# A gating norm moved ahead of a weight split, one weight unit loaded earlier, and accumulator banks taken in three groups

## The chip, the cores and the metric

The kernel runs on one core of one Trainium2 chip. The metric is the time of one execution in microseconds, measured on the device. Three runs of the kernel before gave a median of 531.14 us (531.03 to 531.18). A difference of about 0.2% is the smallest that such a measurement can tell from no change.

## The reference

One decoder layer on 256 tokens of width 1024, in float32. `h` is the running sum.

```python
h = h + 0.5 * swiglu(rmsnorm(h, ffn1_norm), ...)          # hidden width 2816
n = rmsnorm(h, mix_norm)
z = n @ w_in                                              # q, k, v, u, gv, 512 columns each
attn = causal attention over 8 heads of 64 (256 tokens are one block)
zg = gelu(z[..., 1536:])                                  # u and gv
gm = u * (tril(w_s) @ layernorm(gv) + b_s)                # in chunks of 128 tokens, 8 groups
gates = sigmoid(n @ w_gate + b_gate)                      # 2048 columns
merged = gates[:, :1024] * (attn @ w_branch_attn) + gates[:, 1024:] * (gm @ w_branch_gmlp)
h = h + merged @ w_out
h = h + 0.5 * swiglu(rmsnorm(h, ffn2_norm), ...)
out = rmsnorm(h, final_norm)
```

## The kernel before, in words

Every weight is read once, in units of 1 MB, in the order in which TensorE uses them (the list `units`, lines 107 to 116): first FFN, then two units each of q, k, gv, u and v, eight of the gates, four of the branches, four of the output projection, second FFN. A unit arrives as two halves of 512 KB in a ring of seven raw buffers (`fetch_to`, line 131, issued on SyncE's queue, SP). `split_half` (line 141) turns each half into a high and a low part of a reduced float format: a copy on ScalarE (line 195), then a subtraction on VectorE (line 197). The split weights lie in a ring of four units (`wp`). Each product is three matmuls, high by high, high by low and low by high (`mm3`, lines 190 to 192).

`chunk` (line 347) asks `unit` (line 156) for its weights; with `ALONE` this writes out the splits of everything up to three units ahead before the matmuls of the current one, and `split_half` in turn writes out loads up to seven halves ahead. So the place of a `chunk` call in the program also sets where the splits of a later unit stand among the instructions of ScalarE and VectorE, and where loads stand in SP's queue. TensorE and SP run in the program's order throughout, and in this part ScalarE and VectorE do too (`in_order`). Each engine therefore waits at its first instruction that is not ready, and everything behind waits with it.

The stage around the first two edits, with the place of the splits that each call writes out:

- `hold[0] = 2 * mv` (line 516) keeps `fetch_to` from loading any half of v until line 664 clears it. In between, SP writes the queries and keys to DRAM for a transposition (lines 652 and 656), reads them back (658 and 661) and loads the norm's gain and bias (662 and 663). Then line 665 loads v and the first gates.
- Line 666, second half of gv: the splits of v's first unit. Line 668: gelu of gv on ScalarE, two instructions.
- Line 669, first half of u: the splits of v's second unit. Line 671: `layer_norm` (line 638) of gv, twice. Each is five VectorE instructions and one power on GpSimd (line 646) between the third and the fifth.
- Line 674: ScalarE copies the queries that came back. Line 675, second half of u: the splits of the first gate unit. Line 677: gelu of u, two instructions.
- Lines 679 and 680: scores on TensorE (line 556), with the mask added on VectorE (line 563). Line 681, `spatial`: eight products on the normed gv (line 605), which run as 16 small matmuls. Line 682: first half of v.

PSUM has eight banks, handed out in turn, so a new bank waits for the reader of the bank taken eight before. `spatial`'s two banks were u's; v's two were those of the first scores.

The third edit is in `down_features` (line 254), which serves the first FFN's second product (line 514) and the output projection (line 756). It takes all eight banks. For the first unit (i equal to 0) it goes through the banks in groups, here six and then two, and within a group makes all high matmuls (line 164) of the unit's two rows of blocks before the low ones (line 169), by `by_passes` (line 171). At the output projection the eight banks were last those of `merge` (line 724): banks 4 to 7 are the four products `pa` of its last loop, which VectorE reads one after another at line 740, with lines 741 and 742 between them.

Of the kernel before, what the change touches and what calls it, by code (L numbers as in the profile page):

```python
# [23 lines left out]
KB = D // P  # L24
# [21 lines left out]
def block_kernel(ctx, tc, t, out):  # L46
# [11 lines left out]
    def bank(name):  # L58
        return psum.tile([P, 512], F32, tag="ps", name=name)
# [40 lines left out]
    def add_units(name, n):  # L100
        first = len(units)
        units.extend((name, i) for i in range(n))
        return first
# [6 lines left out]
    mq, mk, mgv, mu, mv = (add_units(name, 2) for name in ("q", "k", "gv", "u", "v"))  # L110
# [10 lines left out]
    hold = [None]  # L121
# [19 lines left out]
    def split_half(later=False):  # L141

        i, hf = divmod(done_to[0], 2)
        if hf == 0:
            unit_tile(i)
        fetch_to(done_to[0] + RAW)
        done_to[0] += 1
        w, sl = parts[i], half(i, hf)
        return split(w[:, sl, 0, :], w[:, sl, 1, :], raws.pop((i, hf)), later)
# [6 lines left out]
    def unit(i, ahead=PAIRED):  # L156
        split_to(i + 1 + ahead)
        return parts[i]
# [12 lines left out]
    def by_passes(sides, ks=range(KB), K=KB):  # L171


        for k in ks:
            if k < K - 1:
                for ps, of in sides:
                    (sh, _), both = of(k)
                    mm_high(ps, sh, both, k == 0, False)
        for k in ks:
            for ps, of in sides:  # L180
                (_, sl), both = of(k)
                mm_low(ps, sl, both)
        if K - 1 in ks:
            for ps, of in sides:
                (sh, _), both = of(K - 1)
                mm_high(ps, sh, both, False, True)

    def mm3(ps, st, mv_, first, last):
        (sh, sl), (mh, ml) = st, mv_
        nc.tensor.matmul(ps, sh, mh, start=first, stop=False)  # L190
        nc.tensor.matmul(ps, sh, ml, start=False, stop=False)  # L191
        nc.tensor.matmul(ps, sl, mh, start=False, stop=last)  # L192
# [7 lines left out]
    def alloc_T(name, tags):  # L200

        return [act.tile([P, 4, 2, S], F32R, tag=tag, name=f"{name}{c}") for c, tag in enumerate(tags)]
# [4 lines left out]
    def block_of(nT, k):  # L207
        return both_of(nT, k)[:, 0, :], both_of(nT, k)[:, 1, :]
# [7 lines left out]
    def square(hh, pair, name, tag=None):  # L216

        if pair == 0:
            squares[name] = act.tile([P, KB, S], F32, tag=tag, name=f"sq{name}")
        two = slice(2 * pair, 2 * pair + 2)  # L220
        nc.scalar.activation(squares[name][:, two, :], hh[:, two, :], AF.Square, scale=D ** -0.5)

    def token_sums(name, engine=nc.vector):

        sq = squares[name]
        for n in (4, 2, 1):
            engine.tensor_add(sq[:, :n, :], sq[:, :n, :], sq[:, n:2 * n, :])

    def sum_parts(name):
        sq = squares[name]  # L230
        squares[name] = tmp.tile([P, 2, S], F32R, tag="hg", name=f"sqp{name}")
        split(squares[name][:, 0, :], squares[name][:, 1, :], sq[:, 0, :])
# [21 lines left out]
    def down_features(i0, n_units, both_of_k, scale, gain, nT, name, free, near, behind):  # L254

        acc = [bank(f"acc{name}{c}") for c in range(KB)]
        K = 2 * n_units  # L260

        def blocks(cs, ks):
            def of(c):
                def at(k):
                    w, sl = parts[i0 + k // 2], slice(c * P, (c + 1) * P)
                    return (w[:, k % 2, 0, sl], w[:, k % 2, 1, sl]), both_of_k(k)
                return at
            by_passes([(acc[c], of(c)) for c in cs], ks, K)

        far = n_units - near  # L270
        for i in range(far):
            unit(i0 + i, ALONE if i == far - 1 else PAIRED)

            for cs in ((range(KB - 2), range(KB - 2, KB)) if i == 0 else (range(KB),)):
                blocks(cs, (2 * i, 2 * i + 1))
            for then in behind[i:i + 1]:
                then()

        def low_part(c):
            hi, low = block_of(nT, c)  # L280
            nc.vector.scalar_tensor_tensor(low, h[:, c, :], gain[:, c:c + 1], hi.bitcast(F32),
                                           op0=ALU.mult, op1=ALU.subtract)

        lows = []
        for c in range(KB):
            blocks([c], range(2 * far, K))
            for q in range(2):
                nc.vector.scalar_tensor_tensor(h[:, c, :], acc[c][:, q * S:(q + 1) * S], scale, h[:, c, :],  # L290
                                               op0=ALU.mult, op1=ALU.add)
            nc.scalar.activation(block_of(nT, c)[0], h[:, c, :], AF.Identity, scale=gain[:, c:c + 1])
            if c:
                low_part(c - 1)
            if c in (4, KB - 1):
                lows.append(split_half(True))
            if c % 2:
                square(h, c // 2, name, free)
        low_part(KB - 1)
        for rest in lows:  # L300
            rest()
        token_sums(name)
        sum_parts(name)
# [43 lines left out]
    def chunk(i0, nT, name, c, us=range(2), ps=None):  # L347


        if ps is None:  # L350
            ps = [bank(f"{name}_{c}{j}") for j in range(NT)]
        for u in us:
            w = unit(i0 + 2 * c + u, ALONE)
            for k in range(4):
                for j in range(NT):
                    st = tuple(p[:, j * P:(j + 1) * P] for p in block_of(nT, 4 * u + k))
                    mm3(ps[j], st, (w[:, k, 0, :], w[:, k, 1, :]), u + k == 0, u == 1 and k == 3)
        return ps
# [15 lines left out]
    class Hidden:  # L374
# [44 lines left out]
        def rest(self):  # L419

            last = NC // 2
            def first():
                self.leave(NC - 1)
                self.arrive(last - 1)
            return [first, lambda: self.settle(last - 1), lambda: self.arrive(last), lambda: self.settle(last)]
# [85 lines left out]
    nT2 = alloc_T("n2", ("nA", "nB"))  # L511

    with in_order():
        down_features(f1d, FB // 2, lambda k: hidden.aT[:, k], 0.5, gain2, nT2, "2", "nD", 2, hidden.rest())

        hold[0] = 2 * mv
        psq = chunk(mq, nT2, "q", 0)
        rs2 = token_factors("2")
        mixed = act.tile([P, 2 * FB, S], F32, tag="aT", name="mixed")
# [118 lines left out]
        def layer_norm(j):  # L638
            st = small.tile([P, 6], F32, tag="st", name=f"st{j}")
            nc.vector.bn_stats(st, gv[:, j, :])  # L640
            mvr = small.tile([P, 2], F32, tag="mvr", name=f"mvr{j}")
            nc.vector.bn_aggr(mvr, st)
            ve = small.tile([P, 1], F32, tag="ve", name=f"ve{j}")
            nc.vector.tensor_scalar(ve, mvr[:, 1:2], EPS, None, op0=ALU.add)
            r = small.tile([P, 1], F32, tag="lnr", name=f"lnr{j}")
            nc.gpsimd.tensor_tensor(r, ve, nhalf, op=ALU.pow)
            nc.vector.scalar_tensor_tensor(gv[:, j, :], gv[:, j, :], mvr[:, 0:1], lng, op0=ALU.subtract, op1=ALU.mult)
            nc.vector.scalar_tensor_tensor(gv[:, j, :], gv[:, j, :], r, lnb, op0=ALU.mult, op1=ALU.add)
# [17 lines left out]
        chunk(mgv, nT2, "gv", 0, [1], psgv)  # L666
        for j in range(NT):
            nc.scalar.activation(gv[:, j, :], psgv[j], AF.Gelu_apprx_tanh, scale=rs2[j])
        psu = chunk(mu, nT2, "u", 0, [0])
        for j in range(NT):  # L670
            layer_norm(j)

        qT = qk[:, 0].rearrange("p (k t) -> p k t", k=4)
        nc.scalar.copy(qT.rearrange("p k (q c) -> p q k c", c=32), q_back.rearrange("p q (k c) -> p q k c", c=32))
# [73 lines left out]
        for hp in range(4):  # L748
# [5 lines left out]

        nT3 = alloc_T("n3", ("nC", "nD"))
        down_features(mo, 4, lambda k: both_of(mT, k), 1.0, gain3, nT3, "3", "aT", 1,
                      [lambda: settle(2), lambda: settle(3)])
        hidden = Hidden("f2")
# [146 lines left out]
```

## Time and profile before

| | |
|---|---|
| median of three runs | 531.14 us |
| the profiled execution, its own time | 532.47 us |
| its span, first to last instruction | 530.7 us |
| TensorE busy | 518.9 us, 98% of the span |
| VectorE busy | 356.8 us, 67% |
| ScalarE busy | 264.0 us, 50% |
| moved by DMA | 124.72 MB, 235 GB/s over the span |
| mean granted clock of TensorE | 0.995 |

The profile is of one execution. Engines are PE (TensorE), PEld (its weight loads, which overlap its matmuls), DVE (VectorE), ACT (ScalarE), POOL (GpSimd) and SP (SyncE, whose queue issues most DMAs). A granted clock of 1.00 is 2.4 GHz and one of 0.50 is 1.2 GHz. In a timeline, a row gives start, duration, engine, line, operation, output and inputs, shapes and count, and in brackets the idle time before it and what ended that. Matmuls are pipelined: a row's duration is longer than the step from one start to the next.

### The profile page before, as it was taken

What the parts mean: (1) busy time and instruction counts of PE and PEld (TensorE: products, weight loads), DVE (VectorE), ACT (ScalarE), POOL (GpSimd) and SP (SyncE); (2) the same over time, 40 slices, a digit from 0 to 9 for tenths busy, and PEclk for the clock granted to TensorE, in tenths of its full rate; (3) what the DMA queues carried; (4) which work ended last, traced back from release to release, by engine and by line L of the source; (5) the groups of instructions that cost most, each with busy time, mean ns of one, the idle gap of its engine ahead of it and who ended that gap; (6) DMA issues with size and microseconds to landing.
All of it is one profiled execution on the core that took longest, in us unless ns stands there. A gap on an engine that the chain in (4) does not pass through costs nothing.

```text
span 530.7 us, 6854 instructions
## 1 busy us (share of the span) xinstructions
PE 518.9 (98%) x2490; PEld 435.3 (82%) x2490; DVE 356.8 (67%) x501; ACT 264.0 (50%) x366; POOL 12.2 (2%) x20
## 2 busy tenths in 40 slices
PE   8999999999999999979999999999999999999995
PEld 6888888888888888868888898888888888888884
DVE  6886666675454689179976776988875765575424
ACT  7755354544344367194646422667534544463402
POOL 0010000000000001010000000001000000000002
PEclk9999999999999999998999999999999999999999
DMA  8998598978668236976699755829789879677302
GB/s 316 375 339 283 160 342 273 258 229 266 192 205 290 81 105 216 291 301 233 174 331 329 251 181 162 299 103 308 240 220 335 245 273 319 191 237 251 117 0 79
DMA packets 61937, 124.72 MB, mean 235 GB/s; under 512 B 11472, under 2 KB 35536, under 8 KB 61776
## 3 DMA queue, kind: packets, MB, share of 16 engines
q1 hardware_dynamic: 61616, 123.97, 72.0%
q8 instruction: 19, 0.31, 0.2%
q10 hardware_dynamic: 288, 0.33, 0.2%
q14 instruction: 14, 0.11, 0.1%
HBM read 112.21 MB, written 12.06 MB: 234 GB/s over the span
## 4 chain that ended last, share of the span: by engine, by line
PE 83%; DVE 6%; DMA 4%; issue 3%; ACT 2%; SPq 1%; POOL 0%; POOLq 0%; DVEq 0%; ACTq 0%
PE f L192 14%; PE f L191 14%; PE f L190 14%; PE acc L164 10%; PE acc L169 5%; PE acch L192 4%; PE acch L191 4%; PE acch L190 4%; DVE w L197 3%; PE g L191 3%; PE g L192 3%; PE g L190 3%; DMA raw<-in_v 1%; ACT w L195 1%; SPq L364 1%
## 5 line engine op out<-in xcount | busy, mean ns | idle before, releaser
L197 DVE TENSOR_TENSOR w<-raw,w 128x1024 fp32r<-128x1024 f32 x180 | 211.6, 1218 | 81.9 <-ACT w L195 81.8
L195 ACT CAST w<-raw 128x1024 fp32r<-128x1024 f32 x180 | 179.3, 1048 | 99.7 <-PE f L192 49.0
L192 PE MATMUL f<-w,n 128*128 128x512 f32 x336 | 130.8, 389 | 0.0
L190 PE MATMUL f<-w,n 128*128 128x512 f32 x336 | 130.8, 389 | 0.0
L191 PE MATMUL f<-w,n 128*128 128x512 f32 x336 | 130.8, 389 | 0.0
L191 PEld LDWEIGHTS f<-w,n 128*128 128x128 f32 x336 | 63.1, 188 | 13.2
L190 PEld LDWEIGHTS f<-w,n 128*128 128x128 f32 x336 | 63.1, 188 | 13.1
L192 PEld LDWEIGHTS f<-w,n 128*128 128x128 f32 x336 | 63.1, 188 | 13.0
L164 PE MATMUL acc<-f1h,w 128*128 128x512 f32 x176 | 43.4, 391 | 0.0
L164 PEld LDWEIGHTS acc<-f1h,w 128*128 128x128 f32 x176 | 31.9, 188 | 5.8
L191 PE MATMUL acch<-w,f2h 128*128 128x512 f32 x84 | 32.7, 389 | 0.0
L192 PE MATMUL acch<-w,f2h 128*128 128x512 f32 x84 | 32.7, 389 | 0.0
L190 PE MATMUL acch<-w,f2h 128*128 128x512 f32 x84 | 32.7, 389 | 0.0
L191 PE MATMUL g<-w,n 128*128 128x512 f32 x64 | 24.9, 389 | 0.0
L192 PE MATMUL g<-w,n 128*128 128x512 f32 x64 | 24.9, 389 | 0.0
L190 PE MATMUL g<-w,n 128*128 128x512 f32 x64 | 24.9, 389 | 0.0
L169 PEld LDWEIGHTS acc<-f1h,w 128*128 128x128 f32 x176 | 23.5, 191 | 1.5
L169 PE MATMUL acc<-f1h,w 128*128 128x256 f32 x176 | 23.9, 282 | 0.0
L389 ACT ACTIVATE f2s<-f,rstd 128x256 f32<-128x256 f32 x22 | 10.2, 472 | 27.2 <-PE f L192 27.0
L391 DVE SCALAR_TENSOR_TENSOR f2a<-f,rstd,f2s 128x256 f32<-128x256 f32 x22 | 10.3, 475 | 18.2 <-ACT f2s L389 18.1
L389 ACT ACTIVATE f1s<-f,rstd 128x256 f32<-128x256 f32 x22 | 10.3, 473 | 24.3 <-PE f L192 22.8
L190 PEld LDWEIGHTS acch<-w,f2h 128*128 128x128 f32 x84 | 15.8, 188 | 3.3
(172 smaller groups left out, 627.7 us busy)
## 6 DMA issues: line engine op xcount, KB each, us to landing
raw<-in_f SPq DMA_DIRECT2D x84, 512.0 KB, 6.4
raw<-in_f1d SPq DMA_DIRECT2D x22, 512.0 KB, 5.9
raw<-in_f2d SPq DMA_DIRECT2D x22, 512.0 KB, 6.1
raw<-in_gate SPq DMA_DIRECT2D x16, 512.0 KB, 6.5
raw<-in_out SPq DMA_DIRECT2D x8, 512.0 KB, 5.4
f1way<-f1t SPq DMA_DIRECT2D x11, 256.0 KB, 6.5
f2way<-f2t SPq DMA_DIRECT2D x11, 256.0 KB, 5.2
front<-in_first SPq DMA_DIRECT2D x7, 384.0 KB, 6.0
```

The costliest lines, as they stand in the source:

```text
L164: nc.tensor.matmul(ps, st, both.rearrange("p two n -> p (two n)"), start=first, stop=last)
L169: nc.tensor.matmul(ps[:, n:], st, both[:, 0, :], start=False, stop=False)
L190: nc.tensor.matmul(ps, sh, mh, start=first, stop=False)
L191: nc.tensor.matmul(ps, sh, ml, start=False, stop=False)
L192: nc.tensor.matmul(ps, sl, mh, start=False, stop=last)
L195: nc.scalar.copy(hi, src)
L197: nc.vector.tensor_sub(lo, src, hi.bitcast(F32))
L364: nc.sync.dma_start(to[32 * a:32 * a + 32], squares32[:, :, a, :])
L389: nc.scalar.activation(sg, ps[j][:, :CH], AF.Silu, scale=rs[j])
L391: nc.vector.scalar_tensor_tensor(a, ps[j][:, CH:], rs[j], sg, op0=ALU.mult, op1=ALU.mult)
```

## The change

Three edits. The limit of the held loads goes up by one unit, so the two halves of v's first unit are no longer held. The two layer norms are written ahead of the call that writes out the splits of v's second unit. And the first unit in `down_features` goes through the banks in groups of four, two and two, in place of six and two.

```diff
-            for cs in ((range(KB - 2), range(KB - 2, KB)) if i == 0 else (range(KB),)):
+            for cs in ((range(4), range(4, 6), range(6, KB)) if i == 0 else (range(KB),)):
                 blocks(cs, (2 * i, 2 * i + 1))
...
-        hold[0] = 2 * mv
+        hold[0] = 2 * mv + 2
         psq = chunk(mq, nT2, "q", 0)
...
             nc.scalar.activation(gv[:, j, :], psgv[j], AF.Gelu_apprx_tanh, scale=rs2[j])
+        for j in range(NT):
+            layer_norm(j)
         psu = chunk(mu, nT2, "u", 0, [0])
-        for j in range(NT):
-            layer_norm(j)
```

## Rows read from the trace of the kernel before

**Rows 1.** The view of waits, TensorE alone, the two that are not at the start: who waited, for whom, total us, times, longest.

```profile
PE mix L605 <- DVE mixed L648: 3.4, 1, 3.4
...
PE acc L164 <- DVE mixed L740: 0.6, 1, 0.6
```

**Rows 2.** The chain of work that ended last, from 205 to 245 us: start, duration, what.

```profile
217.91 6.83 DMA raw<-in_v
...
228.40 0.94 ACT w L195
...
230.51 1.22 DVE w L197
231.72 0.61 DVE st L640
...
234.58 0.61 DVE st L640
```

**Rows 3.** TensorE's timeline from 205 to 250 us; the row that starts at 237.78 is from the same view cut at 238.0 to 238.6, which holds eight of the sixteen, and the last row is from the view of the tile `mix` (shortest, median and longest matmul in ns, first and last start).

```profile
219.96 0.39 PE L192 MATMUL gv<-w,n 128*128 128x512 f32 x1
...
230.84 0.39 PE L192 MATMUL u<-w,n 128*128 128x512 f32 x1
231.28 2.96 PE L556 MATMUL sc<-qk 64*128 64x128 f32 x32
237.59 2.73 PE L605 MATMUL mix<-mixed,wsT 128*128 128x128 f32 x16 [3.35 <-DVE mixed L648]
...
237.78 1.06 PE L605 MATMUL mix<-mixed,wsT 128*128 128x128 f32 x8
...
240.37 0.80 PE L190 MATMUL v<-w,n 128*128 128x512 f32 x1
...
242.66 0.39 PE L190 MATMUL v<-w,n 128*128 128x512 f32 x1
...
L605 PE MATMUL mix<-mixed,wsT x16: 275/312/423, 237.6 to 239.9; 128*128 128x128 f32 x16
```

**Rows 4.** The view by stretches of time: stretch, its length, busy time and count of PE, PEld, DVE, ACT and POOL, then the granted clock, the DMA engines' busy share and GB/s.

```profile
239.00:239.50 0.50, 0.50 (x5) 0.50 (x4) 0.50 (x1) 0.00 (x0) 0.00 (x0) 0.50 0.00 0
...
242.50:243.00 0.50, 0.50 (x4) 0.42 (x3) 0.50 (x1) 0.00 (x0) 0.00 (x0) 1.00 1.03 344
...
321.20:323.20 2.00, 1.36 (x7) 0.79 (x6) 1.90 (x6) 1.69 (x2) 0.00 (x0) 1.00 0.66 256
```

**Rows 5.** The timelines of VectorE and of ScalarE from 205 to 250 us.

```profile
203.59 2.35 DVE L197 TENSOR_TENSOR w<-raw,w 128x1024 fp32r<-128x1024 f32 x2
...
236.70 0.75 DVE L648 SCALAR_TENSOR_TENSOR mixed<-mixed,lnr 128x512 f32<-128x512 f32 x1 [0.45 <-POOL lnr L646]
...
239.63 2.61 DVE L563 TENSOR_TENSOR mixed<-sc,mask 128x512 f32<-128x512 f32 x6
...
223.56 1.05 ACT L195 CAST w<-raw 128x1024 fp32r<-128x1024 f32 x1 [11.47 <-DMA raw<-in_v]
...
230.18 1.05 ACT L674 COPY qk<-qback 128x1024 f32<-128x1024 f32 x1
231.13 1.99 ACT L195 CAST w<-raw 128x1024 fp32r<-128x1024 f32 x2
233.02 1.27 ACT L677 ACTIVATE mixed<-u,rstd 128x512 f32<-128x512 f32 x2
```

**Rows 6.** SP's queue from 205 to 250 us; the view by stretches of time around it (columns as in rows 4); and from the view of DMA issues from 195 to 246 us: transfer, count, KB each, median us from issue to landing.

```profile
211.26 0.38 SPq L656 DMA_DIRECT2D qkway<-mixed  x1
...
217.44 2.31 SPq L139 DMA_DIRECT2D raw<-in_v  x4
...
204.00:206.00 2.00, 2.00 (x11) 1.65 (x10) 1.95 (x2) 0.58 (x1) 1.38 (x1) 1.00 0.97 352
...
210.00:212.00 2.00, 2.00 (x10) 1.68 (x9) 2.00 (x4) 2.00 (x3) 0.00 (x0) 1.00 0.00 0
...
qkway<-mixed SPq DMA_DIRECT2D x2, 512.0 KB, 3.0
...
mixed<-in_ln_b SPq DMA_DIRECT2D x1, 256.0 KB, 5.3
```

**Rows 7.** TensorE's timeline at the start of the output projection, and VectorE's beside it.

```profile
321.14 1.33 PE L164 MATMUL acc<-mg,w 128*128 128x512 f32 x5
323.11 1.88 PE L164 MATMUL acc<-mg,w 128*128 128x512 f32 x7 [0.64 <-DVE mixed L740]
...
322.68 0.38 DVE L740 TENSOR_TENSOR mixed<-pa,mixed 128x256 f32<-128x256 f32 x1
...
325.17 0.39 DVE L740 TENSOR_TENSOR mixed<-pa,mixed 128x256 f32<-128x256 f32 x1
```

**Rows 8.** The chain of work that ended last over the whole span, at the first FFN's second product: its first unit, and the start of the second.

```profile
126.13 2.72 PE acc L164 x12
128.85 1.43 PE acc L169 x12
130.29 0.93 PE acc L164 x4
131.22 0.47 PE acc L169 x4
131.69 3.67 PE acc L164 x16
```

More of the change, by code (lines that the diff above doesn't have):

```diff
@@ L668, in block_kernel @@
             nc.scalar.activation(gv[:, j, :], psgv[j], AF.Gelu_apprx_tanh, scale=rs2[j])
-        psu = chunk(mu, nT2, "u", 0, [0])
         for j in range(NT):
             layer_norm(j)
+        psu = chunk(mu, nT2, "u", 0, [0])
         qT = qk[:, 0].rearrange("p (k t) -> p k t", k=4)
```

## The prediction

> **What bounds the kernel now.** The table comes first: TensorE is busy for 98% of the span, so time can only come from the few places where it stands still or runs slowly. The view of waits, filtered to TensorE, has two of them behind the start: 3.4 us before `spatial`, put down to the second layer norm, and 0.6 us at the output projection's first matmuls, put down to VectorE's reads of the last `pa` banks [rows 1]. I then read the first place backwards in the chain of waits. The norm starts at 231.72, right behind the splits of v's second unit on VectorE; those stand behind the splits of v's first unit; and that unit was only issued from 217.44 and landed 6.83 us later [rows 2, 6]. ScalarE stood at that split for 11.47 us until 223.56, with the gelu of gv queued behind it although TensorE had started gv's last matmul at 219.96 [rows 3, 5]. So the late load and the split written ahead of the norm hold up the same norm.
>
> The view by stretches shows a second loss: after the stall the granted clock fell, 0.50 at 239.0 to 239.5, and was 1.00 again from 242.5 [rows 4]. The first sixteen matmuls and the first six of v behind the stall are stretched by it.
>
> **Edit 1 and 2, step by step.** *When v's first unit arrives.* Its two loads are written out at the splits of gv's second unit. A raw buffer is free again seven halves later, so the second load waits for the first split of the pair at 203.59, that is until 204.8 [rows 5]. This is ahead of SP's first write of the queries. The DMA engines then move 352 GB/s until 206 and nothing in 210 to 212 [rows 6]. 1.05 MB at 352 GB/s is 3.0 us, so v lies there by 210. Its split must also wait for the ring buffer of gv's first unit, which TensorE leaves 24 steps before the end of gv: a step is (230.84 - 219.96) / 48 = 0.227 us [rows 3], so 214.7. ScalarE splits it by 216.8 (1.99 a pair) and VectorE by 218 [rows 5], while TensorE is still in gv.
>
> *The norm.* Gelu of gv can follow TensorE at 220.4 and takes the 1.27 us that u's takes [rows 5]. The first norm starts at about 221, and one norm takes 234.58 - 231.72 = 2.86 us [rows 2], GpSimd's power and the wait for it included. Both end at about 226.8, before 237.45 [rows 5]. The norm's bias is issued just before 217.44 and lands 5.3 us later, by 222.6 [rows 6]; the first use is the norm's last instruction, after 223, so it hides.
>
> *What stands behind the norm.* v's second unit now heads the queue at 217.44 and takes the first unit's landing, 224.74 [rows 2]. ScalarE: that split to 225.8, the queries' copy to 226.9, the first gate unit from 228.3 at the latest (it takes the second unit's place in the queue, which ScalarE was splitting at 228.40 [rows 2]) to 230.3, then gelu of u when TensorE ends u at 231.2, to 232.5. VectorE: v's second unit 226.8 to 229.2, the gate unit to 231.6 or 232 at the latest, then the mask adds.
>
> *What is late next.* Scores can start 0.23 after 230.84, at 231.07 in place of 231.28, since the queries' copy is 4 us early. They take 2.96 us, of which some 0.2 overlap the next matmul: to 233.8. `spatial` then needs the norm (226.8, a margin of 7.0 us) and u's banks (gelu, 232.5, a margin of 1.3). v needs the first mask add: its 512 columns are a quarter of the six adds' 2048, so a quarter of 2.61 us: 232 + 0.7 = 232.7 [rows 5] against 235.5, a margin of 2.8. None is late, and TensorE goes through.
>
> *The sum.* From u's last start to v's seventh start the trace has 242.66 - 230.84 = 11.82 us [rows 3]. Without stall and at full clock it is 0.23 for u, 2.75 for the scores (2.96 if nothing overlaps), 16 steps of `spatial`, and 6 x 0.227 = 1.36 for v. The eight `spatial` matmuls of the cut row take 1.06 us, less one's 0.31, over seven steps: 0.107 a step, 1.71 for all. Together 6.05 (6.26), so 5.8 (5.6) us go. I take 5.7. Of these 3.35 are the stall; (240.37 - 237.59) - 1.71 = 1.07 and (242.66 - 240.37) - 1.36 = 0.93 come with it, by the clock and by v's wait for the mask adds; the rest is the earlier start of the scores.
>
> *Costs of these two edits.* The load of v goes ahead of the queries' write. If it pushes that by all of its 3.0 us, the write, 3.0 us long [rows 6], still lands soon after SP's next wait, which is VectorE's transposition until 211.26; what follows in SP's queue is late by 1.5 us at most, against margins of 4 (queries) and 7 (norm). The gates' loads would make gelu of u late by 0.2 at most. So 0, with 0.3 as the upper end. The norm ahead of the split costs VectorE nothing new, the same instructions.
>
> **Edit 3.** At the output projection bank 5 is the sixth to be touched; it is free when VectorE's read at 322.68 ends, at 323.06, and TensorE waits 0.64 us there [rows 7]. With four banks first, TensorE has eight high matmuls of 0.23 and eight low of 1.43 / 12 = 0.12 [rows 8], 2.8 us, until 323.9: bank 5 is free. Banks 4 and 5 take 0.93 + 0.47 to 325.3. Bank 7 is free at 325.17 + 0.39 = 325.56 [rows 7] and wanted one step behind, at 325.5: nothing to 0.1. The gain is 0.6 (0.5 to 0.64), all on TensorE's path. Its VectorE side hangs on TensorE's and DMA's steps before it and moves with them. At the first FFN's second product nothing waited at this place [rows 1]; the last two banks come at the same place in time, and a change of group is free: four high matmuls in 0.93 against sixteen in 3.67 are 0.233 and 0.229 each [rows 8], so under 0.05 either way.
>
> **Total.** 5.7 + 0.6 = 6.3 us. The profiled execution would go from 532.47 to 526.2 and its span from 530.7 to 524.4; it was 1.3 above the median of the runs, which goes from 531.14 to 524.8. Nothing behind gives it back, as far as rows show: no other wait of TensorE is listed [rows 1], and the mask adds, from which softmax and its transfers follow, come at 232 and not 239.63, more than TensorE's gain.
>
> **Rivals.**
>
> *The clock falls anyway.* Scores and `spatial` are short matmuls, and the fall came a microsecond behind the stall's end, not in it: the eight matmuls of the cut row still go at 0.107 a step [rows 3]. Then up to 1.07 + 0.93 = 2.0 us stay: 526.8. Against it: at the output projection TensorE stood for 0.64 us and the clock stayed 1.00 [rows 4]. The Trainium skill ("TensorE: Matmul & The Clock Gate", section "A second HAM failure mode: psum-queue depth-cycling") says that short idle times between groups of matmuls, as banks are cycled, can be enough to swing the clock. By that rule it would be this rival's 526.8; the 1.00 around the 0.64 us speaks against it.
>
> *The wait moves to the gates' load.* If the first gate unit comes no earlier than it was used, 231.13 [rows 5], gelu of u ends at 234.4 and `spatial` starts 0.6 late; v's banks are then no later. Time 525.4; if u's gelu slips another microsecond, 526.4. For it: the DMA queue is full there; against: 1 MB less lies ahead of it.
>
> *The load isn't early.* If something holds v's first unit until 217.44 after all, the norm's move alone acts: gelu ends at 228.4, the norms at 233.5, then four splits of 1.2 us ahead of the mask adds, to 238.3; v starts at 239.6 with the clock fallen, where it was 240.37. 0.7 + 0.6 gained: 529.8. Against: SP has no instruction between the splits of gv and the queries' write that waits long.
>
> *Slower: the queries come too late.* v's megabyte ahead of their write delays write, return and copy, and the scores stall. The copy is needed at 230.0 and could run at 225.8, the returned halves are there earlier still, so it decides from some 4 us of delay and makes the kernel slower from 4 + 6.3, over 10 us: 531.3 at 10.5 us. The size of v's load, 3.0 us, speaks against it. The Trainium skill ("DMA: Bandwidth & Descriptors", section "Queues, rings and completion order") says that each DMA engine takes one queue's descriptors in order; by that rule the delay is the whole 3.0 us, the upper end taken above.
>
> **How the numbers follow.** Forecast 0.75 (own range 524.3 to 525.3), clock 0.10, gates' load 0.07, load not early 0.05, slower 0.03. Predicted 524.8. The range reaches over the clock's rival, 524.1 to 527.2. A measurement of this kernel tells about 0.2%, 1.1 us: faster are the first three and half of the fourth, 0.94; same 0.03; slower 0.03.
>
> **What would show it.** Right: no wait of TensorE for line 648; ScalarE's split of v's first unit at about 215 instead of 223.56; the norms done before 228; granted clock 1.00 from 231 to 243; v's first matmul 4.9 us earlier; no wait for line 740 at the output projection. Wrong: a clock of 0.50 after the scores, a wait of `spatial` for line 677 or of v for line 563, or a new wait between v and the output projection that takes back what was gained.

## The result and the profile after

The changed kernel has a median of 525.95 us (525.60 to 526.22, five runs) against 531.16 us (531.03 to 531.39, five runs) for the kernel before: a ratio of 0.9901, 95% interval 0.9887 to 0.9916. It is 5.2 us faster; 524.8 was predicted, with a range of 524.1 to 527.2. The profiled execution took 526.22 us with a span of 524.5, where 526.2 and 524.4 were predicted. Those are 6.25 and 6.2 us under the profiled execution of before.

The view of waits of the changed kernel, TensorE alone. Both waits for VectorE of [rows 1] are gone; what is left is at the start.

```profile
PE warm L94 <- DVE zeros L91: 1.2, 1, 1.2
PE f L468 <- ACT n L444: 0.2, 1, 0.2
```

TensorE's timeline of the same stretch as [rows 3].

```profile
230.89 0.39 PE L192 MATMUL u<-w,n 128*128 128x512 f32 x1
231.21 2.89 PE L556 MATMUL sc<-qk 64*128 64x128 f32 x32
234.03 2.05 PE L605 MATMUL mix<-mixed,wsT 128*128 128x128 f32 x16
235.84 0.47 PE L190 MATMUL v<-w,n 128*128 128x512 f32 x1
...
237.30 0.40 PE L190 MATMUL v<-w,n 128*128 128x512 f32 x1
```

`spatial` follows the scores without a gap and v follows `spatial`. From u's last start to v's seventh it is 6.41 us, where it was 11.82. The view by stretches (columns as in [rows 4]) has the full clock throughout:

```profile
231.20:241.00 9.80, 9.80 (x72) 8.43 (x72) 8.68 (x12) 6.79 (x17) 0.00 (x0) 1.00 0.80 270
```

How it comes about stands in the timelines of ScalarE, VectorE and SP, against [rows 5, 6]:

```profile
215.00 2.00 ACT L195 CAST w<-raw 128x1024 fp32r<-128x1024 f32 x2 [2.86 <-PE gv L192]
...
219.76 1.37 ACT L668 ACTIVATE mixed<-gv,rstd 128x512 f32<-128x512 f32 x2 [1.46 <-PE gv L192]
225.06 1.05 ACT L195 CAST w<-raw 128x1024 fp32r<-128x1024 f32 x1 [3.93 <-DMA raw<-in_v]
...
220.48 0.69 DVE L640 BATCH_NORM_STATS2 st<-mixed 128x6 f32<-128x512 f32 x1 [2.04 <-ACT mixed L668]
...
222.31 0.75 DVE L647 SCALAR_TENSOR_TENSOR mixed<-mixed,mvr 128x512 f32<-128x512 f32 x1 [0.73 <-DMA mixed<-in_ln_g]
...
226.59 0.75 DVE L648 SCALAR_TENSOR_TENSOR mixed<-mixed,lnr 128x512 f32<-128x512 f32 x1 [0.45 <-POOL lnr L646]
227.26 4.62 DVE L197 TENSOR_TENSOR w<-raw,w 128x1024 fp32r<-128x1024 f32 x4
232.40 2.89 DVE L563 TENSOR_TENSOR mixed<-sc,mask 128x512 f32<-128x512 f32 x6 [0.52 <-PE sc L556]
...
202.43 2.80 SPq L139 DMA_DIRECT2D raw<-in_v  x2
...
213.57 1.80 SPq L364 DMA_DIRECT2D qback<-qkway  x4
```

v's first unit is issued from 202.43, ahead of the queries. Its split now waits for TensorE to leave gv's first unit and runs at 215.0; the gelu of gv follows TensorE; the norms run from 220.48 to 227.3 in front of four splits; and the mask adds wait for TensorE's scores (0.52), not the other way round.

The output projection's first unit, against [rows 7]:

```profile
315.80 2.00 PE L164 MATMUL acc<-mg,w 128*128 128x512 f32 x8
317.64 1.12 PE L169 MATMUL acc<-mg,w 128*128 128x256 f32 x8
318.60 1.09 PE L164 MATMUL acc<-mg,w 128*128 128x512 f32 x4
319.52 0.63 PE L169 MATMUL acc<-mg,w 128*128 128x256 f32 x4
320.00 1.09 PE L164 MATMUL acc<-mg,w 128*128 128x512 f32 x4
320.92 0.64 PE L169 MATMUL acc<-mg,w 128*128 128x256 f32 x4
321.40 2.91 PE L164 MATMUL acc<-mg,w 128*128 128x512 f32 x12
```

It takes 321.40 - 315.80 = 5.60 us from its first matmul to the first of the next unit. In the kernel before, two more rows of the timeline of [rows 7] end the same unit, and it takes 327.66 - 321.14 = 6.52 us:

```profile
324.83 1.59 PE L169 MATMUL acc<-mg,w 128*128 128x256 f32 x12
...
327.66 1.56 PE L164 MATMUL acc<-mg,w 128*128 128x512 f32 x6
```

At the first FFN's second product, where nothing had waited, the unit starts at 126.02 and the next one at 131.59, 5.57 us, where [rows 8] has 131.69 - 126.13 = 5.56.

```profile
126.02 1.98 PE L164 MATMUL acc<-f1h,w 128*128 128x512 f32 x8
...
131.59 3.82 PE L164 MATMUL acc<-f1h,w 128*128 128x512 f32 x16
```

### The profile page after: what moved, and what is told of

It reads as the page before. It is cut to its first block, busy times and chain, and to the rows that moved or that the text cites. A ratio compares the mean times of both kernels' runs of the same rounds, so it can differ in the third digit from the quotient of the medians.

```text
span 524.5 us, 6855 instructions
## 1 busy us (share of the span) xinstructions
PE 516.8 (99%) x2490; PEld 433.8 (83%) x2490; DVE 357.1 (68%) x501; ACT 264.8 (50%) x366; POOL 11.8 (2%) x20
## 4 chain that ended last, share of the span: by engine, by line
PE 97%; DMA 1%; DVE 0%; issue 0%; ACT 0%; POOLq 0%; DVEq 0%; POOL 0%; ACTq 0%
PE f L191 15%; PE f L192 15%; PE f L190 15%; PE acc L164 10%; PE acc L169 5%; PE acch L192 4%; PE acch L191 4%; PE acch L190 4%; PE g L191 3%; PE g L192 3%; PE g L190 3%; PE f L468 1%; PE pg L190 1%; PE pa L192 1%; PE pa L191 1%; PE f L470 1%
```

## The experiments

The runs below were made on three chips; each comparison is between kernels on one chip, or with the kernel before on the same chip. The edits are shown against the kernel before unless another is named.

**The norms moved, the load as before.**

```diff
+        for j in range(NT):
+            layer_norm(j)
         psu = chunk(mu, nT2, "u", 0, [0])
-        for j in range(NT):
-            layer_norm(j)
```

> Only the norms are moved ahead of the splits of v's second unit; v's first unit is still loaded from 217.4 and the groups stay six and two. My theory: gelu of gv still ends at 228.4, the norms end at 233.5, spatial runs without a wait from 234.1; but four splits of 1.2 us now stand between the norms and the mask adds, so v's first matmul waits for the first mask add until about 239, a stall of some 3 us by line 563, with a fallen clock behind it. 1.4 us gained, up to 2.3 if the clock stays: 528.9 to 529.8. Rival: the place of the norms was the cause of the stall, and TensorE goes through: about 526.5.

Measured: 530.98 us against 532.09, ratio 0.9971 (0.9956 to 0.9986), 1.1 us faster; the profiled execution took 529.94. The longest wait of TensorE, and v's start from its timeline:

```profile
PE v L190 <- DVE mixed L563: 2.6, 1, 2.6
...
238.82 0.50 PE L190 MATMUL v<-w,n 128*128 128x512 f32 x1 [2.65 <-DVE mixed L563]
```

The stall before `spatial` is gone, and a new one stands one place further on: v waits for the bank of the first scores, since the mask adds are now behind four splits. The expected start was about 239. The gain of 1.1 us is below the expected 1.4 to 2.3, and its rival (526.5) is out. The clock did not fall behind this stall in the profiled execution, which is the fastest of the eight runs. It seems to have fallen in some of the others: three of them, 530.96 to 531.38 us, have a mean granted clock of 0.993, where no run of a kernel without the stall (thirty, the changed kernel and its variants) is under 0.996.

**The load early, the norms as before.**

```diff
-        hold[0] = 2 * mv
+        hold[0] = 2 * mv + 2
```

> Only the limit of the held loads goes up by one unit; the norms stay behind the splits of v's second unit, and the groups stay six and two. My theory: v's first split moves to about 215 and the gelu of gv to 220, but the norms now stand behind v's second unit's split, which waits for its load until about 225: norms from 228.5 to 234.2, spatial at about 234.3, no stall there. The gate unit's split and the mask adds then end the wait of v's first matmul, at about 237.3 in place of 240.37: a stall of some 1.4 us before v, and 3.0 to 3.9 us gained, 527.3 to 528.2. Rival: the late load was the whole cause and the place of the norms nothing; then v starts at about 236 as in the changed kernel, about 526.5. Second rival: the place of the norms was the cause; then under 1 us is gained.

Measured: 528.15 us against 532.09, ratio 0.9934 (0.9911 to 0.9958). In the profiled execution the only waits of TensorE behind the start are 0.7 us for line 740 and this one:

```profile
PE v L190 <- DVE mixed L563: 0.3, 1, 0.3
```

So the late load was the larger cause: 3.9 us of the gain come with this edit alone. The wait before v is 0.3 and not 1.4 us, because the first half of v's second unit had landed by 223.6, not 225, and the norms ended at 232.8:

```profile
223.57 1.06 ACT L195 CAST w<-raw 128x1024 fp32r<-128x1024 f32 x1 [3.05 <-DMA raw<-in_v]
...
232.10 0.75 DVE L648 SCALAR_TENSOR_TENSOR mixed<-mixed,lnr 128x512 f32<-128x512 f32 x1 [0.45 <-POOL lnr L646]
```

The eight runs fall into two kinds, 527.3 to 528.6 and 530.8 to 531.3, so the kernel was run on two more chips.

> The kernel with the higher limit alone, one more look: its eight runs were of two kinds, near 527.5 and near 531, and the profiled one was of the first kind. Theory: where the norms stand behind v's second split, they hang on when that load lands; in the second kind it lands 2 us or more later than 223.6, so that spatial or v waits for 2 to 3 us and the clock falls behind it. A look at 531 would show a wait of TensorE for line 648 or 563 of over 1.5 us. Rival: the waits are the same 0.3 us and the clock falls with no stall ahead of it. A look at 527.5 again tells nothing.

> The higher limit alone, once more, on the same chip. Theory: it is 1 to 2 us slower than edits 1 and 2 together, since the norms behind v's second split leave the mask adds late (v waits 0.3 to 0.8 us for line 563 in its two looks), and some of its runs are near 531, where a later load lets spatial stall and the clock fall. Rival: with the load early the place of the norms is worth nothing: within 0.3 us of edits 1 and 2.

The first took 527.6 us, with 0.8 us of wait before v. The second has six runs from 526.81 to 528.19, median 527.97, against 532.47 for the kernel before (ratio 0.9910, 0.9892 to 0.9929). On its chip both edits together take 526.75: the place of the norms is worth 1.2 us in the medians once the load is early. The profiled executions put 0.5 to 1.1 us of that into this stage: from u's last start to v's seventh the three with the load alone take 6.92, 7.00 and 7.52 us, and those with both edits 6.41 and 6.42. The one beside both edits, 6.92, also has two waits for line 740, which lie in another stage (what sets them stands under the last experiment):

```profile
PE acc L164 <- DVE mixed L740: 1.4, 2, 0.7
```

Runs near 531 did not come again and none was profiled. Their mean granted clock was 0.993 and 0.994, and 0.996 to 0.999 in the five faster ones, so the clock very likely fell in them, as the theory has it; what TensorE waited for ahead of that stays open.

**Both, without the groups, and the groups alone.**

```diff
-            for cs in ((range(KB - 2), range(KB - 2, KB)) if i == 0 else (range(KB),)):
+            for cs in ((range(4), range(4, 6), range(6, KB)) if i == 0 else (range(KB),)):
```

> Edits 1 and 2 without the groups. My theory: the changed kernel's time plus the 0.6 us of the groups, 526.5, with the 0.6 us wait for line 740 back at the output projection and none before spatial or v. Rival: in the changed kernel VectorE comes to line 740 earlier against TensorE than before, so that the wait would be gone or grown without the groups: 525.9 or over 527.

> Only the three groups of banks, in both places that use the helper. My theory: the 0.64 us before bank 5 at the output projection goes, nothing elsewhere changes: 0.6 us faster, 530.5. Rival: what waits for line 740 there only moves to banks 6 and 7, since VectorE reads them later still: 531.1 and a wait of TensorE for line 740 in the view of waits.

> Edits 1 and 2 without the groups, once more, against the changed kernel on the same chip. Theory: 0.3 to 0.7 us slower than the changed kernel. Rival: no difference that the runs can tell, since the wait only moves to bank 7.

> The changed kernel beside the next three on one chip. In one of its profiled executions bank 7 of the output projection waited 0.39 us for the last read at line 740, in the other not at all. Theory: that read hangs on when the merged blocks come back from DRAM, because the split of the returned block (settle) stands ahead of the reads on VectorE. So the groups' gain is 0.6 us less 0 to 0.4 from run to run. Median 525.6 to 526.2.

Both edits without the groups: 526.71 us against 532.09 (ratio 0.9890, 0.9875 to 0.9906), and on another chip 526.75 against 532.47 (0.9892, 0.9872 to 0.9912). In both profiled executions the wait for line 740 is back, 0.7 and 0.8 us, and there is none before `spatial` or v, as expected. The changed kernel on the second chip: 526.05 (0.9882, 0.9862 to 0.9903). The groups are worth 0.7 us there by the medians, as expected, though the intervals of the two ratios overlap. The groups alone: 531.78 against 532.09, ratio 0.9985 (0.9973 to 0.9998), 0.3 us, less than the 0.6 expected, and no wait for line 740. Its profiled execution shows a possible reason why so little is seen. The first unit of the output projection takes 327.62 - 322.02 = 5.60 us, as in the changed kernel, but the clock fell for longer than in the kernel before. The stall before `spatial` is still there, and the clock fell between 236.5 and 237.0, still inside it, where [rows 3] have eight matmuls at full speed from 237.78:

```profile
322.02 2.00 PE L164 MATMUL acc<-mg,w 128*128 128x512 f32 x8
...
327.62 1.55 PE L164 MATMUL acc<-mg,w 128*128 128x512 f32 x6
...
236.50:237.00 0.50, 0.00 (x0) 0.00 (x0) 0.50 (x1) 0.50 (x1) 0.00 (x0) 0.75 0.02 8
...
237.38 3.75 PE L605 MATMUL mix<-mixed,wsT 128*128 128x128 f32 x16 [3.37 <-DVE mixed L648]
240.79 0.77 PE L190 MATMUL v<-w,n 128*128 128x512 f32 x1
...
243.49 0.44 PE L190 MATMUL v<-w,n 128*128 128x512 f32 x1
...
237.40:243.40 6.00, 6.00 (x22) 5.51 (x23) 6.00 (x10) 0.94 (x1) 0.00 (x0) 0.50 0.54 162
```

From `spatial`'s first matmul to v's seventh it is 6.11 us here, 5.07 in the kernel before [rows 3] and 237.30 - 234.03 = 3.27 in the changed kernel. Part of what is more is v's wait for the mask adds, which comes without the fall too: the next experiment, where the clock stays up behind the same stall, takes 241.87 - 237.50 = 4.37. Against it the fallen clock cost 0.7 us in the kernel before and 1.7 here, so its price is not a fixed one. Four of the twelve runs with the groups alone have a mean clock of 0.990, and none of the twenty-one of the kernel before beside them is under 0.992; why, stays open.

**The stall filled.** The kernel before, with matmuls on zeros that TensorE does while it waits for the norm. They add work that the reference has not, and `spatial` overwrites their result.

```diff
             mix.extend(bank(f"mix{i}") for i in range(2))
+            for i in range(26):
+                nc.tensor.matmul(mix[0][:, :S], zeros[:, :P], zeros, start=True, stop=True)
```

> The kernel before with 26 more matmuls on zeros (256 columns, bfloat16) ahead of spatial, into spatial's own first bank, which spatial then overwrites: some 2.8 us of work for TensorE inside the 3.35 us stall. The stall itself stays. Theory: the clock falls because TensorE stands still, so it now stays at 1.00 through spatial and v; spatial ends about 0.9 us sooner but v still waits for the first mask add, until 240.3; the 0.93 us of slow v matmuls go. So 0.5 to 1 us faster than the kernel before and a narrower spread of its runs. Rival: the clock falls because of the short matmuls of the scores and spatial; then it falls here too and the time is that of the kernel before. If the fill is longer than the stall, TensorE shows no wait there and spatial starts later than 237.6.

Measured: 530.73 us against 531.90, ratio 0.9979 (0.9969 to 0.9989). TensorE's timeline and the stretch around it:

```profile
234.16 3.01 PE L605 MATMUL mix<-zeros 128*128 128x256 bf16 x26
237.50 2.05 PE L607 MATMUL mix<-mixed,wsT 128*128 128x128 f32 x16 [0.33 <-DVE mixed L650]
240.37 0.50 PE L190 MATMUL v<-w,n 128*128 128x512 f32 x1 [0.82 <-DVE mixed L563]
...
241.87 0.39 PE L190 MATMUL v<-w,n 128*128 128x512 f32 x1
...
237.50:240.30 2.80, 2.05 (x16) 1.86 (x16) 2.80 (x4) 1.04 (x1) 0.00 (x0) 1.00 0.18 51
240.30:242.70 2.40, 2.33 (x10) 1.95 (x11) 2.40 (x7) 0.00 (x0) 0.00 (x0) 1.00 0.86 249
```

`spatial` starts when it did (237.50, where [rows 3] have 237.59) and v starts at 240.37, as in [rows 3], held by the mask adds; but the clock is 1.00. The twelve runs bear it out: their mean clock is 0.996 to 0.999, and that of the seventeen of the kernel before 0.991 to 0.996. So the idle TensorE, and not the short matmuls, brought the clock down, and keeping it up is worth 1.2 us in the median (0.6 to 1.6 by the interval). In this stage of the profiled execution it is 0.7 us (4.37 in place of 5.07); what the median has more stays open. The spread is hardly narrower: 530.2 to 532.4 in twelve runs, 531.2 to 534.2 in seventeen of the kernel before.

**The changed kernel against many runs of the kernel before.**

> The changed kernel itself, once more, beside many runs of the kernel before on one chip. Theory: from one profiled execution to the other the change takes 6.25 us, as the sum had it; the median of the timed runs takes only 5.2 because the kernel before differs from run to run in how long and when the clock falls behind its stall, and its profiled execution was at the long end. Then the changed kernel, which has no stall, has runs within 1 us of each other here too, the kernel before has runs spread over 2 us or more, and the difference of the medians lies between 4.7 and 6.3 us. Rival: the sum was too large by a term that the profile shows wrongly; then the difference is 5.2 again with both kernels steady.

Measured: 525.67 us (525.61 to 526.22) against 531.90 (531.22 to 534.20, seventeen runs), ratio 0.9880 (0.9863 to 0.9898): 6.2 us, and the two spreads, 0.6 and 3.0 us, are as expected; the rival, 5.2 again, is out. On the third chip it was 6.4 (526.05 against 532.47). The changed kernel has medians of 525.7 to 526.1 in all three comparisons; the kernel before has 531.16, 531.90, 532.09 and 532.47. That the clock makes the difference between those four is argued and not shown.

**More loaded ahead of the queries.** Against the changed kernel:

```diff
-        hold[0] = 2 * mv + 2
+        hold[0] = 2 * mv + 4
```

> The changed kernel with the held limit another unit higher: both units of v are loaded before the norm's gain and bias, the second between the queries' and the keys' writes. Theory: the transfers of queries, keys, gain and bias come up to 3 us later again, against margins of some 2 us for the norm's use of its gain and bias (which then waits, with 7 us to spare before spatial) and 4 for the queries; v's second split comes sooner. TensorE sees none of it: the time of the changed kernel within 0.3 us. Rival, the slower one of the prediction: the scores wait for the queries or keys, or spatial for the norm, and the time grows by a wait that the view of waits names.

Measured: 526.65 us, ratio 0.9889 (0.9870 to 0.9907), where the changed kernel had 525.67 on this chip. The queries' return is issued at 213.96 and the gain comes late for the norm, but TensorE has no wait between gv and v:

```profile
223.71 0.75 DVE L647 SCALAR_TENSOR_TENSOR mixed<-mixed,mvr 128x512 f32<-128x512 f32 x1 [2.44 <-DMA mixed<-in_ln_g]
```

The mechanism came as expected and was hidden: from u's last start to v's seventh it is 6.41 us, as in the changed kernel. The time is 1.0 above the changed kernel, not within 0.3. Its profile has 0.8 us of waits for line 740 and 0.8 at the start, neither in this stage; the first unit of the output projection takes 6.73 us there, 1.1 more than the 5.60 above. With overlapping intervals, a loss by the edit is not shown.

**The last reads freed from the returned blocks.** In one profiled execution of the changed kernel (the one beside seventeen runs of the kernel before) bank 7 waited after all:

```profile
319.37 0.40 PE L164 MATMUL acc<-mg,w 128*128 128x512 f32 x1
320.16 0.96 PE L164 MATMUL acc<-mg,w 128*128 128x512 f32 x3 [0.39 <-DVE mixed L740]
```

VectorE's last read began at 319.72 there, behind a split of a returned block that came later. Against the changed kernel:

```diff
-                if hf:
-                    settle(j)
+                if hf and j == 0:
+                    settle(0)
...
                 nc.sync.dma_start(by_token(m_way[p]), m_turned[p])
+                if p == 2:
+                    settle(1)
```

> The changed kernel with the split of the second returned merged block (settle 1) written out behind the first pair of reads at line 740 instead of ahead of it. Its result is first used by the second unit of the output projection. Theory: the reads no longer wait for that return, bank 7 is free before it is wanted, and the wait of 0 to 0.4 us goes: 0 to 0.4 us faster than the changed kernel, and no wait of TensorE for line 740. Rival: the second unit then waits for the late split, and the time is the same or up to 1 us longer.

Measured: 525.96 us (0.9877, 0.9857 to 0.9896), where the changed kernel had 526.05. TensorE does not wait for line 740, and the last read, 318.75 to 319.14, is a microsecond ahead of bank 7's first matmul at 320.17. The unit takes 5.60 us, 5.72 in the changed kernel's profiled execution on this chip, which had no listed wait either; the 0.1 us between the medians is not shown.

Fourteen profiled executions together show what sets the length of this unit: how long after TensorE's first matmul of it VectorE starts the first of its four reads at line 740. With groups of six and two the unit took 6.25 to 6.28 us plus that delay in all eight (6.32 at 0.07, 6.52 at 0.25 in the kernel before, 6.90 at 0.63, 7.52 at 1.25). With four, two and two it took some 5.5 us plus the delay (5.72 at 0.23, 6.26 at 0.76, 6.73 at 1.25), and 5.60 in the three where the reads began earlier than the unit. So at a like delay the groups are worth 0.7 to 0.8 us, and the delay is what differs from run to run. At the same delay, first the load alone (the last of its three executions), then `hold[0]` at `2 * mv + 4`:

```profile
315.75 1.09 PE L164 MATMUL acc<-mg,w 128*128 128x512 f32 x4
317.00 0.42 DVE L740 TENSOR_TENSOR mixed<-pa,mixed 128x256 f32<-128x256 f32 x1
323.27 3.83 PE L164 MATMUL acc<-mg,w 128*128 128x512 f32 x16
...
315.49 2.00 PE L164 MATMUL acc<-mg,w 128*128 128x512 f32 x8
316.74 0.42 DVE L740 TENSOR_TENSOR mixed<-pa,mixed 128x256 f32<-128x256 f32 x1
322.22 3.80 PE L164 MATMUL acc<-mg,w 128*128 128x512 f32 x16
```

## Why the prediction was right

*Load, split and norm: right, step by step.* The split of v's first unit was expected at about 215 (215.0), the norms done by 228 (227.3), the scores to 233.8 (234.0), gelu of u early enough, the mask adds by 232 or later. v's first matmul came 4.5 us earlier, where 4.9 were expected. Both parts were needed as the sum took them: the load alone leaves the norms behind the second split (528), the norm's move alone leaves the mask adds behind four splits (531; the rival "the load isn't early" gave the norm's move 0.7 us, and it gained 1.1).

*Its size: 5.7 taken, 5.4 measured between the two profiled executions* (11.82 - 6.41). Each piece was a little long: u to the scores 0.32 (0.23), the scores 2.82 (2.75), `spatial` 1.81 (1.71), v's six steps 1.46 (1.36). At u and v it is the step over a change of shape, 0.32 and 0.31 us where one of 0.227 was taken.

*The groups: right in mechanism, too small in size.* 0.6 was the wait's own length in its row. From start to start the unit went from 6.52 us in the kernel before to 5.60, so 0.92 us went between these two executions. The idle time in the row is counted from the modelled end of the matmul ahead, 0.39 us behind its start, where the next could have started after 0.23: 0.16 more. And the seven matmuls behind the stall took 324.83 - 323.11 = 1.72 us from start to start in place of 7 x 0.229 = 1.60 [rows 7, 8]: 0.12 more. At a like delay of VectorE's reads the groups are worth 0.7 to 0.8 of the 0.92; the rest came because the reads began 0.3 us earlier against TensorE, which the prediction had left out ("moves with them"). That bank 7 would wait "nothing to 0.1" held in some executions; it waited 0.39 and 0.75 in two others. The two errors of size nearly cancel: 5.4 + 0.9 less some 0.1 in the rest of the span are 6.2, against 6.3 predicted. That closeness is luck.

*The step that was off is the last one, from the profiled execution to the median.* 6.3 us, summed in an execution of 532.47, were taken from a median of 531.14. I named the 1.3 us between them and then passed them on to the changed kernel, whose profiled execution is only 0.3 above its median. The runs bear the sum out where the kernel before has more runs: 6.2 and 6.4 us. What varies in the kernel before is, at least in part, the fallen clock: a price of 0.7 or 1.7 us in two executions with the same stall (the second has the groups alone), and 1.2 us in the median when the stall is filled. That the lower median of the first five runs comes from it was not shown.

*The rivals.* The clock did not fall without the stall: it is 1.00 from the scores through the output projection in every profiled execution in which TensorE went through. (Behind TensorE's last matmul it falls to 0.50 in all of them, which costs nothing but moves a run's mean.) Of the Trainium skill's rule ("TensorE: Matmul & The Clock Gate", section "A second HAM failure mode: psum-queue depth-cycling") no run here shows an instance: after waits of 0.3 to 0.8 us the clock stayed at 1.00, and behind 2.65 us too, in one execution; each of these waits stands alone. The gates' load came in time. The queries were pushed: their return was issued at 213.57 and before at 211.74, 1.8 us later where 1.5 at most was expected, and the first norm waited 0.73 us for its gain and 0.66 for its bias, of which the prediction said that it hides. The margin of 7 us hid both. In the changed kernel's other two profiled executions the return was issued at 211.82 and 211.97, and the gain came 0.45 late in one. The slower case needed over 10 us and had 1.8.

## What to carry to other kernels

When a stall has two causes in a row, a late load and an order on an engine that waits in order, removing one moves the wait to the next reader in that order; work out the whole queue of the engine behind the edit, up to the point where TensorE needs it, and count the margin there. Price a TensorE stall by start-to-start distances against an undisturbed stretch, not by the idle time in its row. Where a stall can bring the clock down, its price differs from run to run, so a sum made in one profiled execution should be taken from that execution's time, and the range should hold the distance to the median.

## What was not expected of the hardware

Filling a 3.35 us stall of TensorE with 26 matmuls on zeros made the kernel 1.2 us faster though neither `spatial` nor v started earlier: the granted clock stayed at 1.00 where it had been 0.50. The same stall of 3.4 us was followed by a clock of 0.50 from about 238.7 to 242 in one execution and from about 236.75, still in the stall, to 243.5 in another; a stall of 2.65 us was followed by none in the one execution that was profiled.
